# A hybrid decoder step on one core: PSUM banks lent out by the list scheduler in the order in which it places steps, the last normalisation in other tiles, longer counted durations

## The chip, the cores and the metric

The kernel runs on one core of a Trainium2 chip. The metric is device time in microseconds (us) for one execution. A core has a matrix engine (TensorE, PE in the profile, with its weight loads shown as PEld), a vector engine (VectorE, DVE), a scalar engine (ScalarE, ACT), GpSimd (POOL) and SyncE (SP), whose queue issues almost all of the transfers (DMAs) here. Matmuls write to PSUM, which has eight banks of 128 partitions by 512 float32; everything else lies in SBUF.

## The reference

One layer, 256 prompt tokens and 64 sample tokens (8 sequences of 8), model width 2048, all in float32. The tokens are normalised and projected with one large matrix (2048 by 12,416 columns); branch A is a delta-rule recurrence with 16 heads of 64, branch B a gated linear recurrence with 8 heads of 128. Cut to what matters:

```python
h = rms_norm(x, norm_g);  p = h @ w_in
sh = cur + (prev - cur) * shift_mu                       # token shift of r, k, v, wd, ad
decay = exp(-exp(-softplus(-(w0 + tanh(wd) @ w2)) - 0.5));  a = sigmoid(a0 + ad @ a2)
kk = k * k_k / |k * k_k|;  k = k * (1 + (a - 1) * k_a)
# branch A, per token and head:
S = S * w - (S kk)(kk * a)^T + v k^T ;  y = S r
y_a = ((y - mean) * rsqrt(var + GN_EPS)) * ln_w + ln_b   # the "last normalisation"
y_a = (y_a + sum(r * k * r_k) * v) * silu(p_za)
# branch B, per token and head:
S = diag(g) S + k v^T ;  o = S^T q ;  y_b = rms_norm(o) * hg_g * silu(p_zb)
merged = sigmoid(p_ga) * (y_a @ proj_a) + sigmoid(p_gb) * (y_b @ proj_b)
y = rms_norm(x + merged @ w_out) * final_g               # and all end states are returned
```

## The kernel before, in words

**Streams.** A large float32 product is made of three products of float32r parts: each weight tile of 1024 rows by 128 columns is loaded (`raw`), ScalarE rounds it to `whi`, VectorE subtracts to get `wlo`, and PE multiplies `whi` with the high and low part of the activations (`hhi`, `hlo`) and `wlo` with `hhi`. So each half tile of 128 output columns is one DMA of 512 KB, one ScalarE and one VectorE operation of 1024 columns, and 24 matmuls of 128x128 by 320 tokens, written to one of two PSUM tiles `mps`. Such matmuls are called streams below. There are three buffers each of `raw`, `whi` and `wlo`.

**Stages.** First the tokens are normalised and transposed. Then comes the recorded stage (lines 1431 to 1497): 71 tiles of `w_in` (eight for each of eight head pairs, in the order r, k, v, za, q, f, i, zb, then NFILL + NLATE = 7 gate tiles, of which the last three are stored to DRAM and fetched again later; the tile of the decay ranks is multiplied ahead of it) and, between them, the two recurrences of each pair. Then gate tiles and the two projections (lines 1524 to 1551, `ppa`, `ppb`), which need `ya` and `yb` of all pairs, split into `yah`, `yal` and so on (lines 1514 to 1523). Last the output projection (`po`) and the final norm.

**The planner.** In the recorded stage no instruction is issued when it is written. The class `Recorder` (lines 79 to 323) collects them: `add` (97) gives each a counted duration `cost` and a latency `lat` until its result can be used; `link` (179) finds who depends on whom; `order` (233) then plays the engines forward with these counts. On PE it takes a ready small step before a stream (with some rules about array modes, lines 264 to 280), on the others it takes by rank, and weight splits by due time. The resulting order is issued engine by engine (line 1496), and the framework adds the semaphores. So the chip executes each engine's list strictly in the planned order: where the plan believed a result to be ready earlier than it is, the engine stands still. Counted: a matmul's result after 215 ns plus a margin of 400 ns; a DMA 5500 ns; a DMA from or to the DRAM scratch `scr` 3300 ns, or 4600 ns if its rows have 1024 elements.

**One head pair of branch A** (`rwkv`, lines 810 to 1196). The front: decay and rate (`lora_w`, `lora_a` through `wst`, `ast` on PE), key norm (`uQ`, `uK`), a prefix sum `B` (`uB`), exponentials `ex` (`uE`) and `e2` (`uS`), products `bk2` and `arp`. Then ten matmuls of all score blocks (`arp`, `bk2`) into four PSUM tiles, masked into `g2`. A triangular inverse follows: `nd` (tag `big`) goes to DRAM (`prompt_[0]`), the sample part `dns` too (`sample_[0]`), and both come back spread over partitions, as `U` (columns 0 to 1023 of the tile `ww`) and `eighth` (columns from 1056, line 954); VectorE solves 8x8 blocks in `ww`; the result goes to DRAM (`scr<-xc`) and back (`ye`, `xt` in `uQ`, `yes`), becomes `yz`, and PE multiplies (`a<-yz,uE`, then `a<-ww,uQ`). Then four chunks run one after the other (`pr`, `pu`, `pd`, lines 1062 to 1104), the samples beside them, `py` sums the output, and the last normalisation (lines 1176 to 1196) subtracts the mean (`jr_cent`), squares, averages (`jr_mean`) and writes `ya`.

**Tiles and banks.** SBUF tiles come from `ring` (731) by tag: one buffer each, mostly. Several names share a tag: `uE` is `ex`, then `M`, then `yc` of the last normalisation; `uB` is `B`, then `sq`; `uA` is `a`, then `sg`; `uK` is `kk`, `pw_`, `yt` and `rv`; and `uS`, `uB`, `pp` lie within `ww`. Six PSUM banks are given out by the same `ring` in written order: three in turn to branch A (tag `a`), two to branch B (tag `b`), one to `y` (`own[0]`, `pr`, `py`). Of three `a` banks, the one for a product of the next pair is thus fixed by how many were asked for before it in the text.

Of the kernel before, what the change touches and what calls it, by code (L numbers as in the profile page):

```python
# [9 lines left out]
F32 = mybir.dt.float32  # L10
F32R = mybir.dt.float32r
# [3 lines left out]
PSUM = bass.MemoryType.PSUM  # L15
# [4 lines left out]
NT = NP_ + NS  # L20
# [20 lines left out]
NFILL = 4  # L41
NLATE = 3
BUFS = {"r": 1, "k": 1, "v": 1, "za": 2, "q": 2, "f": 2, "i": 1, "zb": 1}

# [5 lines left out]
class Op:  # L50
    __slots__ = ("eng", "fn", "args", "kw", "cost", "lat", "uses", "mode", "passes", "cols", "stream",
                 "succ", "npred", "ready", "rank", "block", "margin", "wait", "port", "hold", "dma", "n", "group")

# [25 lines left out]
class Recorder:  # L79
    APART, MARGIN, WAIT, OVER = 10, 400, 6000, 45  # L80
    AHEAD, SLIP = 300, 0
    LAT = {"PE": 215, "V": 40, "S": 40, "G": 65, "Y": 0}
    DRAIN = {"V": 85, "S": 100, "G": 65}

    def __init__(self, engines, is_big):
        self.real, self.ops, self.spans, self.is_big = engines, [], {}, is_big
        self.block, self.wait, self.group = None, 0, None

# [8 lines left out]
    def add(self, eng, name, fn, args, kw):  # L97
        o = Op()
# [5 lines left out]
        for d in out.shape[1:]:  # L104
            free *= d
        o.uses = []
        for j, x in enumerate(aps):
            t_ = x.tensor
            key = (t_.name, x.offset, tuple(map(tuple, x.ap)))
            if key not in self.spans:  # L110
                self.spans[key] = blocks_of(x) if t_.name.startswith("scr") else span_of(x)
            o.uses.append((*self.spans[key], j == 0, "PSUM" in str(x.space)))
# [29 lines left out]
        elif eng == "V":  # L142
            two = name in ("tensor_scalar", "tensor_copy") and all(not u[5] for u in o.uses)
            o.cost = (free / 2 if two else free) / 0.96 + (150 if two else 157)
            if two:
                o.hold = o.port = True
            if any(tuple(x.shape[1:]) == (1,) and free > 1 for x in aps[1:]):
                o.cost += 55
            if name == "tensor_tensor_scan":
                o.cost = 2 * free / 0.96 + 157  # L150
        elif eng == "S":
            o.cost = (150 if name == "copy" else 200) + free / 1.2
            if name == "copy" and not o.uses[1][5]:
                o.cost += 40
            if any(tuple(x.shape[1:]) == (1,) and free > 1 for x in aps[1:]):
                o.cost += 90 if k.get("func") == AF.Copy or AF.Copy in a else 60
        elif eng == "G":
            o.cost = 950 if "dma" in name else 95 + free * 0.88 if name == "memset" else (330 if name == "tensor_copy" and free > 9 else 200) + free * 1.66
            if "dma" in name:
                o.lat = 4500  # L160
        else:
            o.cost, o.lat = 380, 5500
            if any(u[0].startswith("scr") for u in o.uses):
                o.lat = 4600 if out.shape[-1] == 1024 else 3300
        if eng in self.DRAIN and not o.dma:
            if name == "tensor_reduce":
                n = 1
                for d in aps[1].shape[1:]:
                    n *= d
                o.cost += (n - free) / 0.96  # L170
            if out.shape[0] == 128:
                o.cost -= self.DRAIN[eng]
                o.lat += self.DRAIN[eng]
            else:
                o.cost += 13
        self.ops.append(o)
        return o

    def link(self):
# [53 lines left out]
    def order(self):  # L233
# [12 lines left out]
        at = {}  # L246
        for j, o in enumerate(bigs):
            at.setdefault(o.block, j)
        gone = run_ = 0

        def choose(e):

            q = ready[e]
            now = free[e]
            if e in port:
                held = port["G" if e == "V" else "V"] - self.OVER
                if e == "V" and held > now and port["G"] == free["G"]:

                    held += min((o.cost for o in ready["G"] if o.hold and o.ready <= free["G"] - 40), default=0.0)
                at_ = {o: max(now, o.ready, held if o.port else 0.0) for o in q}  # L260
                t_ = min(at_.values())
            else:
                t_ = max(now, min(o.ready for o in q))
            if e == "PE":
                can = [o for o in q if o.ready <= t_ + 1]
                own = [o for o in can if o.mode == mode and not o.stream]
                part = [o for o in can if o.mode != (128, 128)]
                if mode != (128, 128):
                    near = [o for o in q if o.mode == mode and o.ready <= t_ + 60]
                    pool = own or near or part or can  # L270
# [7 lines left out]
                if o.stream:  # L278
                    o = min((o for o in pool if o.stream), key=lambda o: o.n)
                return max(t_, o.ready), o  # L280
            if e not in port:
# [14 lines left out]
        while left:  # L296
            t_, o = min((choose(e) for e in ready if ready[e]), key=lambda x: (x[0], x[1].eng == "V"))
            ready[o.eng].remove(o)
# [14 lines left out]
            if o.hold:  # L313
                port[o.eng] = start + cost
            free[o.eng] = end = start + cost
            for q, data in o.succ:
                q.npred -= 1
                q.ready = max(q.ready, end + (o.lat + q.margin if data else 0))
                if not q.npred:
                    ready[q.eng].append(q)  # L320
# [4 lines left out]
def hybrid_step(ctx, tc, x_prompt, x_sample, state_rwkv, state_hgrn, state_shift, norm_g, w_in,  # L325
# [397 lines left out]
    pb = rec.enter_context(tc.tile_pool(name="pb", bufs=1))  # L723
    psa = rec.enter_context(tc.tile_pool(name="psa", bufs=1, space=PSUM))
    psb = rec.enter_context(tc.tile_pool(name="psb", bufs=1, space=PSUM))
    psy = rec.enter_context(tc.tile_pool(name="psy", bufs=1, space=PSUM))
    rings = {}
    wide_ = pa.tile([128, 1288], F32, name="ww", tag="ww")
    SHARED = {"uS": 0, "uB": 384, "pp": 768}

    def ring(pool, tag, shape, bufs, dt, size, clear=False):
# [17 lines left out]
        if len(shape) == 2:  # L749
# [3 lines left out]

    SIZES = {"uK": 384, "uS": 384, "uE": 384, "uA": 320, "uB": 384, "uQ": 320, "pp": 256, "big": 512, "s0t": 512, "v": 384,
             "w1": 384, "w2": 320, "w3": 320, "ks": 128, "ket": 256, "o": NT}
# [12 lines left out]
    def aps(name="aps"):  # L768
        return ring(psa, "a", [128, 512], 3, F32, None)

    def bps(name="bps"):
        return ring(psb, "b", [128, 512], 2, F32, None)

# [36 lines left out]
    def rwkv(p, r, k, vp, za):  # L810
# [38 lines left out]
        e = at("e", (128, 16))  # L849
        f = at("f", (128, 16))  # L850
        V.tensor_copy(e[:, 0:4], B[:, 31:NP_:64])
# [73 lines left out]
        banks = [aps("pg") for _ in HS]  # L925
        own = [ring(psy, "y", [128, 512], 1, F32, None), aps("pg")]
        side_by_side([((banks[h][:, 128 * ci:128 * ci + 128] if ci < 4 else own[h][:, :128],
# [23 lines left out]
        Y.dma_start(U, prompt_[0].rearrange("(b i) m -> b (i m)", i=32)[:, None].to_broadcast([16, 8, 1024]))  # L951
        pitch, parts_ = wide_.ap[0]
        within = lambda o_, *d: bass.AP(wide_.tensor, wide_.offset + o_, [wide_.ap[0], *d])
        eighth = bass.AP(wide_.tensor, wide_.offset + 1056, [[8 * pitch, 16], [32, 8], [1, 8]])
        Y.dma_start(eighth, sample_[0].rearrange("(b i) j -> b i j", i=8))
# [33 lines left out]
        for h in range(2):  # L989
            for a_ in range(2):  # L990
                Y.dma_start(xt[64 * h:64 * h + 32, 2 * a_:2 * a_ + 2, 0:32],
                            prompt_[1].rearrange("(a h c b r) m -> a h b r c m", a=2, h=2, c=2, b=2)[a_, h, 0])
        yes = at("yes", (64, 2, 8))
        Y.dma_start(yes, sample_[1].rearrange("(h p) j -> p h j", h=2))
# [42 lines left out]
        yh = at("yh", dt=F32R)  # L1037
        yl = at("yl", tag="rl", dt=F32R)

# [3 lines left out]
        states = []  # L1043
        pr = ring(psy, "y", [128, 512], 1, F32, None)
        psr = aps("psr")
# [16 lines left out]
        def chunks():  # L1062
            st_ = None
            for ci in range(4):
# [3 lines left out]
                if st_ is None:  # L1068
                    S.copy(rt[tk, 0], pr[HS[0], 0:64])
                    S.copy(rt[tk, 1], pr[HS[1], 0:64])  # L1070
                    rv = at("rv", (128, 3, 64), tag="uK")
                    S.copy(rv.rearrange("p c v -> p (c v)"), pr[:, 64:256])
# [83 lines left out]

        py = ring(psy, "y", [128, 512], 1, F32, None)
        work = []
# [21 lines left out]
        sums(ps[:, :NT], jr_cent, (yh, yl))  # L1180
        yc = at("yc", (128, 384), tag="uE")[:, :NT]
        S.copy(yc, ps[:, :NT])
        sq = at("sq", tag="uB")
        S.activation(sq, ps[:, :NT], AF.Square)
        sp = parts(sq)
        sg = at("sg", tag="uA")
        sigm(sg, za)
# [301 lines left out]
    with tc.manual_schedule():  # L1489
        book = Recorder({"PE": T, "V": V, "S": S, "G": G, "Y": nc.sync},  # L1490
                        lambda out: out.tensor.name.startswith("mps"))
        real = V, S, G, T
        V, S, G, T, Y = (book.proxy(e) for e in ("V", "S", "G", "PE", "Y"))
        record_all()
        V, S, G, T = real
        for o in book.order():
            o.fn(*o.args, **o.kw)  # L1497

# [217 lines left out]
```

## Time and profile before

| | |
|---|---|
| three runs | 1091.84, 1093.39, 1093.44 us; median 1093.39 us |
| the profiled execution | 1095.93 us, with a span of 1094.1 us from its first to its last instruction |
| mean granted TensorE clock | 0.995 |
| HBM read and written | 154.07 MB and 11.42 MB, 151 GB/s over the span |
| sixteen DMA engines | the hardware queue's packets take 52.4% of their time |

All times of the trace are counted from the first instruction. An engine's busy time is the union of its instructions; PE is pipelined, so that the recorded duration of a matmul is longer than the time until the next one starts. A wait is put down to whoever set the semaphore last. Inside the recorded stage nearly every instruction has line 1497, where the plan is issued; they are told apart by what they write and read: `a<-yz,uE` is a matmul that writes a PSUM tile of ring `a` and reads `yz` and `uE`.

### The profile page before, as it was taken

Reading aid. Unit: us, or ns where it says so; the run is one execution under the profiler, and the core shown is the slowest. Engines: PE = TensorE matmul, PEld = TensorE weight load, DVE = VectorE, ACT = ScalarE, POOL = GpSimd, SP = SyncE. Lnnn points to the kernel's source line nnn. Section 1 sums busy time; section 2 is a strip of 40 time slices with the busy share of each in tenths; the row PEclk is TensorE's granted clock in tenths of the full one; section 3 lists DMA queues with packets and bytes.
Section 4 is the critical chain, followed back from the end, with each engine's and each line's share of the span. In section 5 each row is a group of like instructions: output and inputs, shape, how many; then the busy total and the mean of one; then the engine's idle time right before and its main releaser. Section 6 shows DMA issues by size and latency. Waiting matters only on the chain.

```text
span 1094.1 us, 23029 instructions
## 1 busy us (share of the span) xinstructions
PE 1065.8 (97%) x8828; PEld 1027.6 (94%) x8828; DVE 760.6 (70%) x1640; ACT 706.5 (65%) x1608; POOL 133.3 (12%) x366
## 2 busy tenths in 40 slices
PE   8998999999999999999999999999999999999996
PEld 7998998998999989999989989999999999988885
DVE  8778898888897986997897885644444444446532
ACT  7757968868879959859769777544444444444412
POOL 8510120301210210300210110000000000000000
PEclk9999999999999999999999999999999999999999
DMA  6654554655555455555455555555455555587402
GB/s 197 184 146 125 154 159 121 166 145 152 144 164 141 138 163 140 138 145 159 138 145 155 140 143 164 153 155 159 144 147 154 154 146 146 152 302 247 162 20 96
DMA packets 302353, 166.98 MB, mean 153 GB/s; under 512 B 39261, under 2 KB 291424, under 8 KB 301668
## 3 DMA queue, kind: packets, MB, share of 16 engines
q1 hardware_dynamic: 301876, 164.21, 52.4%
q8 instruction: 69, 1.13, 0.4%
q10 hardware_dynamic: 368, 1.31, 0.3%
q14 instruction: 40, 0.33, 0.1%
HBM read 154.07 MB, written 11.42 MB: 151 GB/s over the span
## 4 chain that ended last, share of the span: by engine, by line
PE 78%; DVE 10%; DMA 4%; ACT 4%; issue 3%; SPq 0%; DVEq 0%; POOL 0%; ACTq 0%
PE mps L1497 30%; PE a L1497 7%; PE mps L389 5%; PE mps L391 5%; PE mps L390 5%; DVE wlo L1497 3%; DMA ww<-scr 3%; PE b L1497 3%; PE po L1589 3%; PE po L1588 3%; PE po L1587 3%; PE ppa L390 2%; PE ppb L389 2%; PE ppb L390 2%; PE ppb L391 2%
## 5 line engine op out<-in xcount | busy, mean ns | idle before, releaser
L1497 PE MATMUL mps<-hhi,wlo 128*128 128x320 f32 x1136 | 357.1, 314 | 1.5 <-DVE wlo L1497 0.8
L1497 PE MATMUL mps<-hlo,whi 128*128 128x320 f32 x1136 | 357.5, 315 | 0.0
L1497 PE MATMUL mps<-hhi,whi 128*128 128x320 f32 x1136 | 357.2, 314 | 0.0
L1497 PEld LDWEIGHTS mps<-hhi,wlo 128*128 128x128 f32 x1136 | 214.6, 189 | 2.7 <-DVE wlo L1497 1.4
L1497 PEld LDWEIGHTS mps<-hhi,whi 128*128 128x128 f32 x1136 | 214.5, 189 | 1.6 <-issue 1.2
L1497 PEld LDWEIGHTS mps<-hlo,whi 128*128 128x128 f32 x1136 | 214.4, 189 | 1.6 <-issue 0.8
L1497 DVE TENSOR_TENSOR wlo<-raw,whi 128x1024 fp32r<-128x1024 f32 x140 | 172.5, 1232 | 21.8 <-ACT whi L1497 20.6
L379 ACT CAST whi<-raw 128x1024 fp32r<-128x1024 f32 x82 | 86.2, 1051 | 147.2 <-PE mps L390 94.0
L380 DVE TENSOR_TENSOR wlo<-raw,whi 128x1024 fp32r<-128x1024 f32 x82 | 100.5, 1225 | 111.1 <-ACT whi L379 110.9
L1497 ACT CAST whi<-raw 128x1024 fp32r<-128x1024 f32 x140 | 145.8, 1043 | 42.4 <-PE mps L1497 27.2
L389 PE MATMUL mps<-hhi,whi 128*128 128x320 f32 x400 | 123.6, 309 | 0.0
L390 PE MATMUL mps<-hlo,whi 128*128 128x320 f32 x400 | 123.6, 309 | 0.0
L391 PE MATMUL mps<-hhi,wlo 128*128 128x320 f32 x400 | 123.6, 309 | 0.0
L389 PEld LDWEIGHTS mps<-hhi,whi 128*128 128x128 f32 x400 | 75.1, 188 | 0.0
L390 PEld LDWEIGHTS mps<-hlo,whi 128*128 128x128 f32 x400 | 75.1, 188 | 0.0
L391 PEld LDWEIGHTS mps<-hhi,wlo 128*128 128x128 f32 x400 | 75.1, 188 | 0.0
L1576 DVE TENSOR_TENSOR wlo<-raw,whi 128x1024 fp32r<-128x1024 f32 x32 | 38.5, 1222 | 38.0 <-ACT whi L1575 37.9
L1575 ACT CAST whi<-raw 128x1024 fp32r<-128x1024 f32 x32 | 33.3, 1053 | 47.4 <-PE po L1592 29.7
L1589 PE MATMUL po<-wlo,mhi 128*128 128x512 f32 x128 | 50.0, 391 | 0.0
L1587 PE MATMUL po<-whi,mhi 128*128 128x512 f32 x128 | 50.0, 391 | 0.0
L1588 PE MATMUL po<-whi,mlo 128*128 128x512 f32 x128 | 50.0, 391 | 0.0
L389 PE MATMUL ppa<-yah,whi 128*128 128x320 f32 x128 | 39.7, 310 | 0.5 <-ACT yah L1519 0.5
(429 smaller groups left out, 2045.8 us busy)
## 6 DMA issues: line engine op xcount, KB each, us to landing
raw<-in_w_in_dram SPq DMA_DIRECT2D x194, 512.0 KB
raw<-in_w_out_dram SPq DMA_DIRECT2D x32, 512.0 KB
raw<-in_proj_a_dram SPq DMA_DIRECT2D x16, 512.0 KB
raw<-in_proj_b_dram SPq DMA_DIRECT2D x16, 512.0 KB
s<-in_state_hgrn_dram SPq DMA_DIRECT2D x8, 512.0 KB
ww<-scr SPq DMA_DIRECT2D x8, 512.0 KB
out_dram<-s SPq DMA_DIRECT2D x8, 512.0 KB
s<-in_state_rwkv_dram SPq DMA_DIRECT2D x8, 256.0 KB
```

The lines of the kernel that those rows point to most:

```text
L379: S.copy(hi[:, ks], raw[:, ks])
L380: sub.tensor_sub(lo[:, ks], raw[:, ks], hi[:, ks].bitcast(F32))
L389: T.matmul(dst, hi[:, q, :], xhi[:, k, :], start=(k == 0), stop=False)
L390: T.matmul(dst, hi[:, q, :], xlo[:, k, :], start=False, stop=False)
L391: T.matmul(dst, lo[:, q, :], xhi[:, k, :], start=False, stop=(k == nk - 1))
L1497: o.fn(*o.args, **o.kw)
L1575: S.copy(hi, raw)
L1576: V.tensor_sub(lo, raw, hi.bitcast(F32))
L1587: T.matmul(pt, h, hi, start=first, stop=False)
L1588: T.matmul(pt, l, hi, start=False, stop=False)
L1589: T.matmul(pt, h, lo, start=False, stop=end)
```

## The change

It has three parts, all in the recorded stage.

**Banks.** The six PSUM banks are six tiles `bank0` to `bank5`. `aps` (now also `bps`, and the `y` tiles) returns no bank but a numbered loan, an address in an imaginary tensor. While `order` runs, a PE step whose loan has no bank yet can be placed only if a bank is idle: `entry` looks at the steps that ask, takes them by rank, skips those that still have an unplaced step ahead of the loan (`asked`) or that are ready only later than 1500 ns from now (`SOON`), and keeps back as many banks as a step or a side-by-side group asks for. When the step is placed, its loan gets the bank that came free first; after the loan's last step the bank is idle again. `emit` puts the real bank's address in when the instruction is issued.

**Tiles.** The last normalisation no longer uses `uE`, `uB` and `uA`: `yc` and `sq` lie in `bk`, `sg` in `big`; the rounded square reuses `yh` and `yl`, and `yl` moves from `rl` to the tag `fd`. `rv` moves from `uK` to `pp`, `yes` to `dns`, and `f` gets two buffers. `ww` grows from 1288 to 1312 columns, and `eighth` is written as a slice of the tile and no more as an address built by hand; it covers the same elements.

**Counts.** A scratch DMA counts 4500 ns and no more 3300, with 1024 elements 6500 and no more 4600. Every step of VectorE, ScalarE and GpSimd that is no DMA counts 20 ns more (`SPARE`).

The number and kind of computing instructions stay as they are, except that the split of the square is written out instead of a call of `parts`. The changed lines (those without context; the numbers are lines of the kernel before near which they stand):

```diff
@@ -40 @@
+LOAN = 128 * 512
@@ -78 @@
-    AHEAD, SLIP = 300, 0
+    AHEAD, SLIP, SOON, SPARE = 300, 0, 1500, 20
-        self.block, self.wait, self.group = None, 0, None
+        self.block, self.wait, self.group, self.loans, self.lent = None, 0, None, -1, []
@@ -103 @@
-        o.uses = []
+        o.uses, o.loans = [], set()
+            if t_.name.startswith("bank"):
+                n, off = divmod(x.offset, LOAN)
+                o.loans.add(n)
+                o.uses.append((f"loan{n}", *span_of(self.moved(x, off))[1:], j == 0, True))
+                continue
@@ -161 @@
-                o.lat = 4600 if out.shape[-1] == 1024 else 3300
+                o.lat = 6500 if out.shape[-1] == 1024 else 4500
+            o.cost += self.SPARE
@@ -175 @@
+    def moved(self, x, off, home=None):
+        home = home or self.lent[0]
+        return bass.AP(home.tensor, home.offset + off, [list(d) for d in x.ap])
+    def emit(self, o):
+        def real(x):
+            if not (hasattr(x, "tensor") and x.tensor.name.startswith("bank")):
+                return x
+            n, off = divmod(x.offset, LOAN)
+            return self.moved(x, off, self.lent[self.home[n]])
+        o.fn(*(real(x) for x in o.args), **{k: real(x) for k, x in o.kw.items()})
@@ -247 @@
+        open_, needs, until = {}, {}, {}
+        for o in self.ops:
+            for n in o.loans:
+                open_[n] = open_.get(n, 0) + 1
+                until[n] = 0.0
+        members = {}
+        for o in self.ops:
+            if o.group is not None:
+                members.setdefault(o.group, set()).update(o.loans)
+        for o in self.ops:
+            for n in o.loans:
+                needs.setdefault(n, o.loans if o.group is None else members[o.group])
+        own, before = {}, {}
+        for o in self.ops:
+            for q, _ in o.succ:
+                before.setdefault(q.n, []).append(o.n)
+            for n in o.loans:
+                own.setdefault(min(needs[n]), set()).add(o.n)
+        ahead, asked = {}, {}
+        for key, mine in own.items():
+            top = max(mine)
+            past, todo = set(), list(mine)
+            while todo:
+                for q, _ in self.ops[todo.pop()].succ:
+                    if q.n <= top and q.n not in past:
+                        past.add(q.n)
+                        todo.append(q.n)
+            todo = list(mine)
+            inner = set(mine)
+            while todo:
+                for n in before.get(todo.pop(), ()):
+                    if n in past and n not in inner:
+                        inner.add(n)
+                        todo.append(n)
+            outer = {n for m in inner for n in before.get(m, ())} - inner
+            asked[key] = len(outer)
+            for n in outer:
+                ahead.setdefault(n, []).append(key)
+        idle = [(0.0, j) for j in range(len(self.lent))]
+        self.home = {}
+        def wanted(o):
+            return [n for n in (o.loans if o.group is None else members[o.group]) if n not in self.home]
+        def entry(q, now):
+            at_, asking = {}, {}
+            for o in q:
+                want = wanted(o)
+                if not want:
+                    at_[o] = o.ready
+                elif not asked[min(needs[want[0]])]:
+                    asking.setdefault(min(want), []).append(o)
+            room, rooms = len(idle), sorted(idle)
+            for some in sorted(asking.values(), key=lambda s_: max((o.rank, -o.n) for o in s_), reverse=True):
+                n = len(wanted(some[0]))
+                first = min(o.ready for o in some)
+                if first > now + self.SOON:
+                    continue
+                if n <= room:
+                    for o in some:
+                        at_[o] = max(o.ready, rooms[n - 1][0] + o.margin)
+                room -= n
+            return at_
-            if e in port:
+            if e == "PE":
+                at_ = entry(q, now) or entry(q, 1e9)
+                q = list(at_)
+                if not q:
+                    return None
+                t_ = max(now, min(at_[o] for o in q))
+            elif e in port:
@@ -262 @@
-                can = [o for o in q if o.ready <= t_ + 1]
+                can = [o for o in q if at_[o] <= t_ + 1]
-                    near = [o for o in q if o.mode == mode and o.ready <= t_ + 60]
+                    near = [o for o in q if o.mode == mode and at_[o] <= t_ + 60]
@@ -277 @@
-                return max(t_, o.ready), o
+                return max(t_, at_[o]), o
@@ -294 @@
-            t_, o = min((choose(e) for e in ready if ready[e]), key=lambda x: (x[0], x[1].eng == "V"))
+            t_, o = min(filter(None, (choose(e) for e in ready if ready[e])), key=lambda x: (x[0], x[1].eng == "V"))
+            for n in wanted(o):
+                idle.sort()
+                self.home[n] = idle.pop(0)[1]
@@ -313 @@
+            for key in ahead.get(o.n, ()):
+                asked[key] -= 1
+            for n in o.loans:
+                open_[n] -= 1
+                until[n] = max(until[n], end + o.lat)
+                if not open_[n]:
+                    idle.append((until[n], self.home[n]))
@@ -721 @@
-    psa = rec.enter_context(tc.tile_pool(name="psa", bufs=1, space=PSUM))
-    psb = rec.enter_context(tc.tile_pool(name="psb", bufs=1, space=PSUM))
-    psy = rec.enter_context(tc.tile_pool(name="psy", bufs=1, space=PSUM))
+    psl = rec.enter_context(tc.tile_pool(name="psl", bufs=1, space=PSUM))
+    lent = [psl.tile([128, 512], F32, name=f"bank{j}", tag=f"bank{j}") for j in range(6)]
-    wide_ = pa.tile([128, 1288], F32, name="ww", tag="ww")
+    wide_ = pa.tile([128, 1312], F32, name="ww", tag="ww")
@@ -751 @@
-    SIZES = {"uK": 384, "uS": 384, "uE": 384, "uA": 320, "uB": 384, "uQ": 320, "pp": 256, "big": 512, "s0t": 512, "v": 384,
+    SIZES = {"uK": 384, "uS": 384, "uE": 384, "uA": 320, "uB": 384, "uQ": 320, "pp": 256, "fd": NT, "big": 512, "s0t": 512, "v": 384,
@@ -766 @@
-        return ring(psa, "a", [128, 512], 3, F32, None)
-    def bps(name="bps"):
-        return ring(psb, "b", [128, 512], 2, F32, None)
+        book.loans += 1
+        at_ = lent[0]
+        return bass.AP(at_.tensor, at_.offset + book.loans * LOAN, [list(d_) for d_ in at_.ap])
+    bps = aps
@@ -847 @@
-        f = at("f", (128, 16))
+        f = at("f", (128, 16), bufs=2)
@@ -923 @@
-        own = [ring(psy, "y", [128, 512], 1, F32, None), aps("pg")]
+        own = [aps("py"), aps("pg")]
@@ -949 @@
-        pitch, parts_ = wide_.ap[0]
-        eighth = bass.AP(wide_.tensor, wide_.offset + 1056, [[8 * pitch, 16], [32, 8], [1, 8]])
+        eighth = wide_[0:128:8, 1056:1312].rearrange("p (i x) -> p i x", x=32)[:, :, 0:8]
@@ -990 @@
-        yes = at("yes", (64, 2, 8))
+        yes = at("yes", (64, 2, 8), tag="dns")
@@ -1035 @@
-        yl = at("yl", tag="rl", dt=F32R)
+        yl = at("yl", tag="fd", dt=F32R)
-        pr = ring(psy, "y", [128, 512], 1, F32, None)
+        pr = aps("py")
@@ -1068 @@
-                    rv = at("rv", (128, 3, 64), tag="uK")
+                    rv = at("rv", (128, 3, 64), tag="pp")
@@ -1154 @@
-        py = ring(psy, "y", [128, 512], 1, F32, None)
+        py = aps("py")
@@ -1178 @@
-        yc = at("yc", (128, 384), tag="uE")[:, :NT]
+        ends = bk.rearrange("p c k -> p (c k)")
+        yc, sq = ends[:, :NT], ends[:, NT:2 * NT]
-        sq = at("sq", tag="uB")
-        sp = parts(sq)
-        sg = at("sg", tag="uA")
+        S.copy(yh, sq)
+        V.tensor_sub(yl, sq, yh.bitcast(F32))
+        sp = yh, yl
+        sg = at("sg", tag="big")
@@ -1490 @@
+        book.lent = lent
-            o.fn(*o.args, **o.kw)
+            book.emit(o)
```

More of the change, by code (lines that the diff above doesn't have):

```diff
@@ L51 @@
     __slots__ = ("eng", "fn", "args", "kw", "cost", "lat", "uses", "mode", "passes", "cols", "stream",
-                 "succ", "npred", "ready", "rank", "block", "margin", "wait", "port", "hold", "dma", "n", "group")
+                 "loans", "succ", "npred", "ready", "rank", "block", "margin", "wait", "port", "hold", "dma", "n", "group")
 def span_of(ap):
```

## The prediction

> **What bounds the kernel now.** I read the page first, then the busy time of each engine in the three parts of the run, then PE's waits in the recorded stage, then each wait's surroundings in the timeline.
>
> ```profile
> span 1094.1 us, 23029 instructions
> PE 1065.8 (97%) x8828; PEld 1027.6 (94%) x8828; DVE 760.6 (70%) x1640; ACT 706.5 (65%) x1608; POOL 133.3 (12%) x366
> ```
>
> ```profile
> 0.00:28.70 28.70, 23.54 (x130) 21.49 (x131) 23.57 (x51) 21.29 (x40) 23.43 (x54) 1.00 0.63 189
> 28.70:678.00 649.30, 635.68 (x6187) 619.58 (x6186) 542.37 (x1343) 507.60 (x1300) 109.84 (x313) 0.99 0.54 149
> 678.00:1094.10 416.10, 406.54 (x2515) 386.53 (x2513) 194.69 (x247) 177.60 (x268) 0.00 (x0) 1.00 0.51 156
> ```
>
> The columns after the length are the busy times of PE, PEld, DVE, ACT and POOL. The change touches the middle part alone, from 28.7 to 678.0 us. There PE works 635.68 of 649.30 us, and VectorE is next with 542.37, so PE bounds the stage. The change removes no matmul, so what it can win here is PE's idle time, 649.30 - 635.68 = 13.6 us, and what hangs on it. Who causes it:
>
> ```profile
> PE a L1497 <- ACT yz L1497: 7.9, 4, 2.9
> PE a L1497 <- DVE rl L1497: 1.6, 1, 1.6
> PE a L1497 <- DVE bks L1497: 1.4, 1, 1.4
> PE mps L1497 <- DVE wlo L1497: 0.8, 1, 0.8
> PE a L1497 <- POOL yz L1497: 0.8, 1, 0.8
> PE mps L1497 <- issue: 0.6, 1, 0.6
> PE a L1497 <- DVE st L1497: 0.2, 1, 0.2
> ```
>
> Each row is waiter, releaser, total, number, longest. In eight of these ten single waits PE stands at a small step (`a`) whose vector or scalar operand comes late, five times at the first product after the inverse's way through DRAM (`yz`: 7.9 + 0.8 = 8.7 us). These are not shortages of streams. PE's list put a small step there because the plan counted its operand as ready; the chip, which can't reorder, waits. The plan is too early, and by how much shows at pair 0:
>
> ```profile
> 68.24 0.57 SPq L1497 DMA_DIRECT2D ww<-scr  x1
> 73.79 0.53 SPq L1497 DMA_DIRECT2D ww<-scrs  x1
> ...
> 77.19 0.19 DVE L1497 TENSOR_TENSOR big<-ww 128x30 f32<-128x30 f32 x1 [3.02 <-DMA ww<-scrs]
> 96.32 0.68 PE L1497 MATMUL a<-yz,uE 128*128 128x128 f32 x4 [2.93 <-ACT yz L1497]
> 404.62 1.19 PE L1497 MATMUL a<-yz,uE 128*128 128x128 f32 x4 [2.42 <-ACT yz L1497]
> ```
>
> ```profile
> SPq L1497 <- DMA ww<-scr: 40.9, 8, 6.0
> ```
>
> `U` is issued at 68.24; `eighth` leaves only at 73.79, because SP waits for `U` to land (40.9 / 8 = 5.1 us for each pair, with the later weight loads queued behind it), though the two fill different columns. The first solve starts at 77.19, 77.19 - 68.24 = 9.0 us after `U` was issued. The plan counts 380 + 4600 ns = 5.0 us there. It is 4.0 us early, and PE's wait of 2.93 us at 96.32 is what is left of that.
>
> **Waits long enough also cost clock.**
>
> ```profile
> 97.00:100.45 3.45, 3.45 (x15) 3.25 (x14) 3.32 (x13) 1.39 (x5) 0.17 (x1) 0.51 0.73 213
> 404.20:407.65 3.45, 3.02 (x12) 3.06 (x13) 3.11 (x8) 1.70 (x6) 0.40 (x2) 0.51 0.43 130
> ```
>
> Around the two longest waits (2.93 and 2.42 us) the granted clock is 0.51 for 3.45 us. That loses (1 - 0.51) times PE's busy 3.45 and 3.02 us: 1.7 + 1.5 = 3.2 us. After the shorter waits (up to 1.6 us) nothing of the kind shows, so I count these 3.2 us as hanging on the long ones. That they have another cause is a rival below.
>
> **Are the pairs serial?** This decides whether PE, freed of waits, still has streams to do.
>
> ```profile
> 120.12 0.31 PE L1497 MATMUL a<-yh,jr_cent 128*128 128x320 f32 x1
> 120.82 0.31 PE L1497 MATMUL a<-lora_w,wst 128*128 128x320 f32 x1
> ```
>
> ```profile
> L1497 SPq DMA_DIRECT2D scr<-big x32: 327/422/434, 63.5 to 608.5; - x32
> L1497 DVE SCALAR_TENSOR_TENSOR v<-dif,cols,pad x16: 274/379/504, 53.1 to 566.0; 128x256 f32<-128x256 f32 x8, 128x64 f32<-128x64 f32 x8
> L1497 DVE TENSOR_TENSOR ya<-uE,uA x8: 491/492/495, 126.7 to 678.3; 128x320 f32<-128x320 f32 x8
> POOL uE L1497 <- DVE ya L1497: 38.7, 7, 9.2
> ```
>
> Pair 1's first product (`lora_w`) comes 0.7 us after pair 0's last normalisation began (`jr_cent`): the `a` bank in turn is free only then. Its `ex` waits further for pair 0's `ya`, since both use `uE` (GpSimd waits 38.7 us in seven times). So a pair starts when the one before ends. The inverse's DMAs recur every (608.5 - 1.3 - 63.5) / 7 = 77.7 us (1.3 us for the three issues of 0.42 us between a pair's first and last), the input v every (566.0 - 0.4 - 53.1) / 7 = 73.2 us. The chain of pairs is 4.5 us a pair slower than the streams, and falls behind them by 32 us over the stage. The seven gate tiles at the end are the cover, used up to the last: the last `ya` starts at 678.3, and the last stream has started by 678.0, where the stage is cut. If PE's idle time went and the chain stayed, PE would only wait at the end. Both must go together.
>
> **The change part by part.**
>
> *Counts.* The way through DRAM counts four scratch DMAs in a row (`nd` out, `U` in, `xc` out, `ye` in): 1.9 + 3 x 1.2 = 5.5 us more. The plan was 4.0 us early, so the product with `yz` should now be placed behind enough streams that its operand is there; the streams in between hide this. I take the 8.7 us of `yz` waits down to 1.0: -7.7. The five other causes (1.6 + 1.4 + 0.8 + 0.6 + 0.2 = 4.6 us) were operands late by 0.2 to 1.6 us. 20 ns for each of the some dozens of steps in a row before them are about that size, so half goes: -2.3. With the two long waits the slow clock goes: -3.2. What the counts cost: the 20 ns on 1343 VectorE steps make 26.9 us, 542.37 + 26.9 = 569 of 649 us in the plan, still below PE, so no wait of PE is planned for VectorE's sake.
>
> *Banks and tiles.* They let pair p+1's front run beside pair p's tail: `ex`, `B`, `a` and `kk` are no longer held by `yc`, `sq`, `sg`, `rv`, and no bank is fixed by the text. What still holds pair p+1 back is `arp`, `g2` and `uv`, which pair p reads until `py`, just ahead of 120.12. Now the scores go out as `nd` some 77.7 - (120.12 - 63.5) = 21 us after that. If only `arp` and the ten matmuls have to follow, I estimate a gain of 10 us, and 4.5 are enough to keep pace with the streams. This gives nothing by itself: it is what lets the sum above be collected at the end.
>
> *New waits.* A bank's next writer waits for its last reader, and the order of loans rests on counted times. In the list above no wait is for a bank. The bounds are 0 and the 8.7 us that the plan's worst error costs now; two pairs interleaved are new, but the nearest row is 0, so I take +2.0. How often PE changes between small steps and streams may shift either way: of PE's 635.68 us, 16.1 have no weight load beside them (619.58), and a fifth of that, 3 us, bounds it on both sides. I take 0.
>
> *`eighth` as a slice.* If the framework now sees that it is apart from `U`, SP no longer stands still for 5.1 us, and the solves start about 3.4 us earlier (77.19 - 73.79, its own landing). If not, all stays. It is off the bound either way, as long as the pairs overlap: 0, with a wait of PE of up to 9.0 - (0.38 + 6.5) = 2.1 us a pair if it stays. The 1.0 above takes half a chance of a part of that.
>
> *After the stage.* PE's first projection waits 0.5 and 0.4 us for the split of `ya`, itself behind the last gate tile's store. That stays: 0.
>
> ```profile
> PE ppa L389 <- ACT yah L1519: 0.5, 1, 0.5
> PE ppa L390 <- DVE yal L1520: 0.4, 1, 0.4
> 685.10 2.61 ACT L1519 CAST yah<-ya 128x640 fp32r<-128x640 f32 x4 [2.33 <-DMA scrg<-f]
> ```
>
> **Sum:** -7.7 - 2.3 - 3.2 + 2.0 = -11.2 us. The profiled execution (1095.93, 1.8 us outside its span) would become 1084.7; it is 2.5 us above the median, so the median of 1093.39 becomes 1082.2.
>
> **Rivals.**
>
> *The slow clock stays (6%).* The two stretches may have a cause of their own and come again: the gain is 3.2 us smaller, 1085.4. For it: two cases are few. Against it: both begin within 1 us of the end of the two longest waits of the stage (96.32, 404.62). [...]
>
> *Half (15%).* `eighth` still waits for `U` and four pairs still wait about 1 us at `yz`, or new bank waits take 4 us more than I count: about -6, 1087.4. For it: SP's wait is the framework's doing, not the plan's.
>
> *Waits only move (11%).* The plan is changed everywhere, and its errors show up at other places for the same 13.6 us: 1093.4. For it: the waits by `rl`, `bks` and `st` have nothing to do with scratch DMAs. Against it: they are a third of the idle time.
>
> *The chain gets longer (14%).* If the pairs remain serial, by `arp`, `g2` and `uv`, each pair is planned 5.5 us later, 4.0 of which the chip needed anyway; 1.5 us a pair, and about 2 us for some hundred steps of a pair at 20 ns, make 3.5 x 8 = 28 us at the last `ya`, with the streams used up: 1121. It decides once pair p+1 wins less than 3.5 us by starting earlier. Against it: 38.7 us of waiting for `uE` alone goes, and the `lora_w` row shows the front waiting for a bank. [...]
>
> **The numbers.** My forecast has 54% (1077 to 1087). If all 13.6 + 3.2 + 0.9 us went, it would be 1075.7, the low end; the high end, 1093, takes in the half gain and part of no change, and leaves out the longer chain and a rest of no change. A measurement of this kernel can tell 0.2% (2.2 us) from no change. Faster: 54 + 6 + 15 = 75%; same 11%; slower 14%.
>
> **What would show it.** Right: PE idle below 5 us in the recorded stage, no clock of 0.5 in it, `lora_w` of pair p+1 on PE well ahead of pair p's `jr_cent`, the inverse's DMAs every 73 to 75 us, and the last `ya` some us ahead of the last gate tile. Wrong: PE waiting for a reader of a bank, a gap at the end of the stage before `ppa`, or `yz` waits as before.

## The result and the profile after

The changed kernel takes 1078.66 us (median of four runs, 1077.21 to 1080.13) against 1093.41 us, a ratio of 0.9867, 95% interval 0.9848 to 0.9885. That is 14.75 us less; 11.2 were forecast.

Busy time of each engine in the three parts of the changed kernel (after the length: PE, PEld, DVE, ACT, POOL, granted clock, DMA share, GB/s):

```profile
0.00:26.80 26.80, 20.86 (x130) 18.30 (x131) 23.18 (x51) 20.65 (x37) 24.44 (x54) 1.00 0.68 202
26.80:661.30 634.50, 630.12 (x6188) 618.15 (x6187) 541.64 (x1344) 504.96 (x1304) 98.21 (x313) 1.00 0.56 151
661.30:1077.50 416.20, 406.92 (x2515) 386.45 (x2513) 195.01 (x246) 177.56 (x268) 0.00 (x0) 0.99 0.52 157
```

The recorded stage went from 649.30 to 634.50 us, 14.8 less. The last part is the same (416.10 and 416.20). The first is 1.9 us shorter, which isn't the change: the stage begins at 26.8 to 27.9 in every other run told of here, with the old planner too; the profiled run of before had a late start. Of the 14.8 us, 9.2 are PE's idle time (13.6 to 4.4) and 5.6 its busy time. PE's waits in the stage:

```profile
PE bank L198 <- issue: 3.4, 2, 2.1
PE bank L198 <- ACT rhs L198: 0.6, 2, 0.3
PE bank L198 <- POOL fd L198: 0.4, 1, 0.4
```

```profile
99.74 0.25 PE L198 MATMUL bank<-uv,g 128*32 128x64 f32 x2 [0.30 <-ACT rhs L198]
```

All rows of `yz`, `rl`, `bks`, `wlo` and `st` are gone. The two waits behind `rhs`, 0.6 us in all, are for a bank's reader: the matmul `bank<-uv,g` waits until ScalarE's copy `rhs<-bank` is done, and it doesn't read `rhs`. Most of what is left stands in the first row: two waits for which the profile has no releaser (the last section says what they go with). Behind the longer one (2.15 us) clock is lost too, as this stretch of the windows view shows after the wait that ends at 330.49:

```profile
330.49 0.22 PE L198 MATMUL bank<-ket 128*32 128x32 f32 x2 [2.15 <-issue]
```

```profile
330.90:334.30 3.40, 3.40 (x15) 3.40 (x16) 1.51 (x8) 1.68 (x7) 0.00 (x0) 0.50 0.02 5
```

Half of 3.40 us, 1.7, is lost there; before it was 3.2. So 1.5 of the 5.6 us of busy time are clock. For the other 4.1 the profile names nothing. Recorded matmuls overlap (a small one of 0.27 us starts 0.11 us after the one before), so by my estimate an operand late by 0.1 us can delay and yet leave no idle time behind; I take the 4.1 us for such waits, but no view shows them one by one. How often PE changes between streams and small steps is not the cause: by the matmul records of the stage it does so 570 times before and 576 times after.

The pairs, in PE's timeline and in the rows by tile:

```profile
83.00 0.31 PE L198 MATMUL bank<-lora_w,wst 128*128 128x320 f32 x1
124.53 0.40 PE L198 MATMUL bank<-yh,jr_cent 128*128 128x320 f32 x1
```

```profile
L198 SPq DMA_DIRECT2D scr<-big x32: 327/424/1462, 59.8 to 590.9; - x32
L198 DVE SCALAR_TENSOR_TENSOR v<-dif,cols,pad x16: 265/376/486, 59.5 to 577.8; 128x64 f32<-128x64 f32 x8, 128x256 f32<-128x256 f32 x8
L198 DVE TENSOR_TENSOR ya<-bk,big x8: 481/491/734, 132.2 to 658.3; 128x320 f32<-128x320 f32 x8
```

Pair 1's first product now comes 41.5 us ahead of pair 0's last normalisation, where it came 0.7 us after it. The inverses recur every (590.9 - 1.3 - 59.8) / 7 = 75.7 us (77.7 before), and the last `ya` starts 3 us before the stage ends. And at pair 0 SP no longer stands between the two transfers, and the first solve starts 7.5 us after `U` is issued instead of 9.0 (SP's and VectorE's timelines):

```profile
64.83 0.56 SPq L198 DMA_DIRECT2D ww<-scr  x1
65.45 0.59 SPq L198 DMA_DIRECT2D ww<-scrs  x1
...
72.36 0.18 DVE L198 TENSOR_TENSOR big<-ww 128x30 f32<-128x30 f32 x1
```

It is not sooner in every pair: over all eight the first solve starts on average 8.7 us after `U` is issued, and 8.0 before; in seven of the eight VectorE works without a pause until the solve begins, so the plan and not the landing sets the time.

### The profile page after: what moved, and what is told of

The parts are those of the page before. It is cut to its first block, busy times and chain, and to the rows that moved or that the text cites. A ratio compares the mean times of both kernels' runs of the same rounds, so it can differ in the third digit from the quotient of the medians.

```text
span 1077.5 us, 23000 instructions
## 1 busy us (share of the span) xinstructions
PE 1057.9 (98%) x8828; PEld 1022.9 (95%) x8828; DVE 759.8 (71%) x1640; ACT 703.2 (65%) x1608; POOL 122.6 (11%) x366
## 4 chain that ended last, share of the span: by engine, by line
PE 96%; DVE 1%; ACT 1%; issue 1%; DMA 1%; POOL 0%; DVEq 0%; ACTq 0%
PE mps L198 47%; PE bank L198 11%; PE mps L493 5%; PE mps L492 5%; PE mps L491 5%; PE po L1693 3%; PE po L1691 3%; PE po L1692 3%; PE ppb L492 2%; PE ppb L493 2%; PE ppb L491 2%; PE ppa L493 2%; PE ppa L492 2%; PE ppa L491 2%; PE po L1697 1%; PE po L1696 1%
## 5 line engine op out<-in xcount | busy, mean ns | idle before, releaser
L492 PE MATMUL ppa<-yal,whi 128*128 128x320 f32 x128 | 39.6, 310 | 0.4 <-DVE yal L1624 0.4
```

The source lines that it names most:

```text
L492: T.matmul(dst, hi[:, q, :], xlo[:, k, :], start=False, stop=False)
```

## The experiments

The theory: the longer counts take PE's waits away, and lent banks with new tiles let the pairs overlap, so that this can be collected. The rivals: the counts do it alone, or the overlap does. Each run has its own runs of the kernel before beside it on the same chip, so ratios are what can be compared between rows. "Period" is that of the inverses, from each run's own row of `scr<-big`.

| run | banks | tiles | 20 ns | scratch counts | `ww` | us | ratio (95%) | period |
|---|---|---|---|---|---|---|---|---|
| before | turns | old | no | old | 1288 | 1093.41 | 1 | 77.7 |
| changed | lent | new | yes | long | 1312 | 1078.66 | 0.9867 (0.9848, 0.9885) | 75.7 |
| e1 | turns | old | yes | long | 1288 | 1134.62 | 1.0376 (1.0361, 1.0392) | 84.3 |
| e2 | lent | new | no | old | 1312 | 1087.07 | 0.9940 (0.9924, 0.9957) | 74.1 |
| e3 | lent | old | yes | long | 1312 | 1116.82 | 1.0217 (1.0202, 1.0232) | 82.6 |
| e4 | turns | new | yes | long | 1312 | 1121.62 | 1.0256 (1.0240, 1.0271) | 82.1 |
| e5 | turns | old | no | old | 1312, slice | 1084.78 | 0.9929 (0.9907, 0.9950) | 76.5 |
| e6 | lent | new | yes | long | 1312, by hand | 1077.75 | 0.9862 (0.9845, 0.9878) | 75.3 |
| e7 | lent | new | no | long | 1312 | 1082.60 | 0.9903 (0.9888, 0.9918) | 74.0 |
| e8 | lent | new | yes | 3000 ns longer | 1312 | 1122.30 | 1.0262 (1.0238, 1.0286) | 83.4 |
| e9 | turns | old | no | old | 1312, by hand | 1084.87 | 0.9923 (0.9906, 0.9940) | 76.6 |
| e10 | lent | new | yes | long | 1288, by hand | 1077.27 | 0.9855 (0.9840, 0.9870) | 75.4 |
| e11 | lent | new | yes | old | 1312 | 1074.57 | 0.9836 (0.9818, 0.9853) | 73.8 |
| e12 | turns | old | yes | old | 1312, by hand | 1104.30 | 1.0070 (1.0053, 1.0088) | 79.4 |

### The counts alone (e1)

```diff
 # the kernel before
-                o.lat = 4600 if out.shape[-1] == 1024 else 3300
+                o.lat = 6500 if out.shape[-1] == 1024 else 4500
         if eng in self.DRAIN and not o.dma:
+            o.cost += self.SPARE        # 20
```

> The kernel before with the longer counts alone (scratch DMAs 6500 and 4500, 20 ns a step); banks, tiles and the hand-built address of eighth as before. My theory (the counts take the waits away, the overlap of the pairs lets the gain be collected): the waits at yz are gone, but the pairs stay serial and each is some 3.5 us longer, so the last ya comes up to 28 us later and PE idles at the end of the recorded stage: 1095 to 1121 us. Rival 'counts do it all': 1079 to 1082 us, with no wait at the end. Rival 'overlap does it all': 1093 us or a little more, the yz waits as before.

It takes 1134.62 us, beyond the slow end of my own range. PE's waits and the inverses:

```profile
PE mps L1498 <- ACT pad L1498: 24.9, 5, 8.9
PE a L1498 <- DVE rl L1498: 10.1, 2, 7.4
```

```profile
L1498 SPq DMA_DIRECT2D scr<-big x32: 306/424/1245, 61.7 to 652.9; - x32
```

The `yz` waits are gone from the list, but the period is 84.3 us. The idle time isn't at the end, as I had it, but in the middle: a stream can't begin because the PSUM tile that it needs hasn't been copied out to `pad`. With r, k and v in one buffer each, the copy waits for the pair before, so streams run dry in five of the eight pairs. The counts alone lose 41 us.

### The overlap without the counts (e2), without the scratch counts (e11), without the 20 ns (e7)

```diff
 # the changed kernel; e11 has the first edit, e7 the second, e2 both
-                o.lat = 6500 if out.shape[-1] == 1024 else 4500
+                o.lat = 4600 if out.shape[-1] == 1024 else 3300
-    AHEAD, SLIP, SOON, SPARE = 300, 0, 1500, 20
+    AHEAD, SLIP, SOON, SPARE = 300, 0, 1500, 0
```

> The changed kernel with the old counts (4600 and 3300, no 20 ns); banks lent and new tiles stay. My theory: the pairs overlap as in the changed kernel (inverse every 75 to 76 us), but the plan is too early again at yz, PE idles 8 to 13 us in the stage: 1084 to 1091 us. Rival 'overlap does it all': within 0.2% of the changed kernel, 1077 to 1081 us. Rival 'counts do it all': 1091 to 1095 us.

> The changed kernel without the 20 ns a step (scratch DMAs stay at 6500 and 4500). My theory: between the changed kernel and the one with all old counts (1087), nearer to the latter if the many small late operands are what the counts mend: 1082 to 1087 us. If the scratch DMAs' counts are what matters: 1077 to 1081 us.

> The changed kernel with the scratch DMAs' old counts (4600 and 3300), the 20 ns a step stay. The 20 ns alone were worth 4 us (1082.6 without them) and all counts together 8.4 (1087.1). If the two add up: 1081 to 1085 us. If, with eighth free of U, the old scratch counts are long enough and the longer ones only lengthen the chain: 1074 to 1079 us.

The two counts don't add up. By the ratios, with the old scratch counts the 20 ns are worth 1.04% of the time of before (0.9940 to 0.9836; 1% is 11 us), with the long ones 0.36% (0.9903 to 0.9867). The long scratch counts gain 0.37% without the 20 ns and cost 0.31% with them. So the fastest of all, 1074.57, has the scratch counts of before; its interval and the changed kernel's just touch. The stage in e2 and in e11:

```profile
26.80:669.80 643.00, 635.27 (x6189) 618.85 (x6188) 542.14 (x1344) 509.75 (x1305) 108.52 (x313) 1.00 0.54 150
```

```profile
26.80:656.50 629.70, 628.61 (x6187) 616.36 (x6187) 542.87 (x1344) 506.77 (x1305) 102.65 (x313) 1.00 0.56 153
```

In both the pairs keep well ahead (74.1 and 73.8 us). In e11 PE idles 1.1 us in the stage, against 4.4 in the changed kernel. Those 3.3 us and the 1.7 of clock make up the 4.8 us by which e11's stage is shorter, and both come from the waits without a releaser (3.4 against 0.2 us). So this shows the long scratch counts to be unnecessary, not that they lengthen anything by themselves. In e2 the loss is not at `yz`, as I had expected (0.2 us there): 6.6 us of idle time more than e11, 4.9 of it waits without a releaser (5.1 and 0.2 us), and 6.7 us of longer busy time, 1.7 of them clock (an estimate, worked out in the last section). So about half of what the 20 ns are worth here (4.9 and 1.7 of 13.3 us in the stage) hangs on waits for which the profile names no late operand. Since only 20 ns was run, it is not shown how much of it another count, or another order, would bring.

### Banks or tiles alone (e3, e4)

```diff
 # e3: the changed kernel with the tiles of before, for instance
+        yc = at("yc", (128, 384), tag="uE")[:, :NT]
-        yc, sq = ends[:, :NT], ends[:, NT:2 * NT]
 # e4: the kernel before with the new tiles, slice and counts; its banks stay
         return ring(psa, "a", [128, 512], 3, F32, None)
```

> The changed kernel with the last normalisation, rv, yl, yes and f back in the tiles of before; banks lent, slice and longer counts stay. My theory: lora_w of the next pair still comes ahead of jr_cent, but its ex waits for ya through uE, so the pairs are about as serial as before and longer: last ya behind the last gate tile, 1085 to 1110 us. If the banks are the whole of the overlap: 1077 to 1081 us.

> The kernel before with the new tiles, the slice and the longer counts, but the banks by turns in written order. My theory: lora_w of the next pair comes only around jr_cent, the front can't run beside the tail, so 1085 to 1105 us with PE idle at the end of the stage. If the tiles are the whole of the overlap: 1077 to 1081 us.

Both are slower than before, by 2.2% and 2.6%, and beyond the slow end of my ranges. Neither half of the overlap is any good without the other while the long counts stand. In e4 PE waits like this, in e3 the same for 16.2 us:

```profile
PE mps L1499 <- ACT pad L1499: 14.9, 5, 7.3
```

### The wait of `eighth` (e5, e6, e9, e10)

```diff
 # e9: the kernel before, one number; e5: this and eighth as a slice
-    wide_ = pa.tile([128, 1288], F32, name="ww", tag="ww")
+    wide_ = pa.tile([128, 1312], F32, name="ww", tag="ww")
 # e6: the changed kernel; e10: this and 1288 columns
-        eighth = wide_[0:128:8, 1056:1312].rearrange("p (i x) -> p i x", x=32)[:, :, 0:8]
+        eighth = bass.AP(wide_.tensor, wide_.offset + 1056, [[8 * wide_.ap[0][0], 16], [32, 8], [1, 8]])
```

> The kernel before with eighth written as a slice of ww (ww widened to 1312 columns) and nothing else. SP should no longer wait for U to land ahead of eighth, and the solves start about 3.4 us earlier in each pair, with the old plan. My theory: a true latency taken off a serial chain shows even without the other parts; the yz waits of 8.7 us and the two slow stretches of 3.2 us mostly go, 1081 to 1088 us. Rival 'off the bound': SP's wait costs nothing and the plan sets the pace, within 0.2% of before, 1091 to 1095.5 us.

> The changed kernel with the address of eighth built by hand again (the wide ww stays). SP waits about 5 us for U in each pair again. My theory: the longer counts cover most of it, and the pairs overlap: PE waits up to 2 us a pair at yz, 1079 to 1087 us. Rival 'off the bound': within 0.2% of the changed kernel, 1077 to 1081 us.

> The kernel before with ww 1312 columns wide and nothing else: the address of eighth is still built by hand, the plan's order is the same. In the run with the changed kernel and the hand-built address SP did not wait for U, so the cause of the wait would be the width (the pattern of 8 rows of 32 from column 1056 ends at 1312), not the way of writing it. Then SP's wait is gone and the time is that of the slice alone, 1082 to 1088 us. If the slice is what frees it: SP's wait of 5 us stays, 1091 to 1095.5 us.

> The changed kernel with ww 1288 columns wide and the hand-built address, so with the false wait back: the solves start some 3 us later in each pair. My theory now: lent banks and new tiles run the pairs side by side and the longer counts cover the late solves, so PE waits little at yz: 1078 to 1084 us. If the freed wait is the main part of the gain: 1084 to 1092 us.

e5 gives 0.9929: a true latency off a serial chain is worth 8 us with no change to the plan. e6 was to bring SP's wait back and did not, so the slice isn't what frees it. e9 changes the width alone, and that is enough (0.9923). SP's and VectorE's timelines in e9:

```profile
66.49 0.57 SPq L1497 DMA_DIRECT2D ww<-scr  x1
67.18 0.53 SPq L1497 DMA_DIRECT2D ww<-scrs  x1
...
72.90 0.19 DVE L1497 TENSOR_TENSOR big<-ww 128x30 f32<-128x30 f32 x1 [0.49 <-DMA ww<-scrs]
```

```profile
PE a L1497 <- ACT yz L1497: 1.9, 3, 1.1
```

The instructions of all engines are those of the kernel before in the same order, and the wait of 40.9 us in eight is gone: 6.4 us from `U` to the first solve at pair 0 instead of 9.0, and 1.9 us of `yz` waits instead of 8.7. The pattern of eight rows of 32 columns from column 1056 ends at 1312; in a tile of 1288 columns it reaches past the row's end, and the framework then takes it to overlap with `U`. That last step is argued; that the width decides is shown.

In the changed kernel none of this matters: e10, with the old width, is as fast as with the new one (1077.27 us, just below my range). Its waits of SP and its timeline at pair 1 say why:

```profile
SPq L198 <- DMA ww<-scr: 4.1, 1, 4.1
```

```profile
136.61 0.54 SPq L198 DMA_DIRECT2D ww<-scrs  x1
137.25 2.10 SPq L198 DMA_DIRECT2D raw<-in_w_in_dram  x2
139.58 0.55 SPq L198 DMA_DIRECT2D ww<-scr  x1
```

The plan issues `eighth` ahead of `U` in seven of eight pairs, so there is one wait where there were eight. Lent banks and new tiles together bring this order, not the longer count: e2, with neither count, has it in seven pairs too, and in e1, e3 and e4, which have the longer counts but at most one of the two, `U` is first in all eight. By which step of the plan they do it, no run shows.

### Longer counts still (e8), and the 20 ns on serial pairs (e12)

```diff
 # e8: the changed kernel
-                o.lat = 6500 if out.shape[-1] == 1024 else 4500
+                o.lat = 9500 if out.shape[-1] == 1024 else 7500
 # e12: e9 with the 20 ns
+            o.cost += self.SPARE
```

> The changed kernel with still longer scratch DMAs: 9500 with 1024 elements, 7500 else, 3 us more for each of four in a row, 12 us a pair. My theory: with the chain already as slow as the streams (last ya 3 us ahead of the last gate tile), 12 us more a pair make the chain the bound, streams run out in the middle of the stage: 1095 to 1150 us. If overlapped pairs hide a longer chain: 1077 to 1083 us.

> The kernel before with ww 1312 columns wide and 20 ns more a step, scratch DMAs counted as before (4600 and 3300); banks by turns and the tiles as before. It is the same as the fastest so far (1074.6: lent banks, new tiles, 20 ns, old scratch counts) less the lent banks and the new tiles. My theory: the pairs are serial and 20 ns for each step make the planned chain about 2 us a pair longer than the 77 us that it has with the width alone, so streams run dry late in the stage and the time is 1085 to 1105 us. If banks and tiles are not needed once the false wait is gone: 1073 to 1079 us.

e8 is the slow rival come true in the changed kernel: 83.4 us a pair, streams waiting for the copy of `zb`, and the projection waiting for the last `ya`:

```profile
PE mps L198 <- ACT zb L198: 9.6, 5, 3.1
PE ppa L491 <- ACT yah L1623: 4.9, 1, 4.9
```

e12 settles what the overlap (lent banks and new tiles together) is for. Serial pairs with the freed wait lose by the 20 ns (0.9923 to 1.0070, 76.6 to 79.4 us a pair), and overlapped ones gain by them (e2 to e11, 0.9940 to 0.9836).

```profile
PE mps L1498 <- ACT pad L1498: 8.1, 2, 5.6
```

## Why the prediction was right, point by point

**The bound and the waits.** Right. PE's idle time in the stage was to fall by 8.0 us net and fell by 9.2; all `yz` waits went (1.0 was left to them), and of the five others' 4.6 us 1.0 is left, at other steps.

**New waits, +2.0.** The size was near (3.4 us), but by luck, since the kind was wrong: they are the waits without a releaser, which the prediction didn't have. For a bank's reader there are 0.6 us, which are among the 1.0 us just named.

**Clock, -3.2.** 1.5 came. The two stretches after the `yz` waits went with them, which speaks against the rival that they stay; a new one follows a new wait. With it one of the signs named for a right prediction failed (no clock of 0.5), and a second one narrowly: the inverses recur every 75.7 us, not every 73 to 75.

**Changes between small steps and streams, 0 within 3 us.** Too narrow: PE's busy time fell by 4.1 us beside the clock, the time without a weight load beside it from 16.1 to 12.0. The number of changes isn't why (570 and 576), so the sum had no term for these 4.1 us. Together with 1.2 us more of idle time and 1.7 less of clock than forecast they are the difference between -11.2 and -14.8.

**The overlap gives nothing by itself and is needed to collect the rest.** Right for the counts, and the experiments show it more sharply than I put it: banks and tiles with the old counts and the new width, e2, are no faster than the width alone, e9; without banks, tiles or both the counts lose 24 to 41 us. But not all of the gain needs the overlap: the width alone takes 6.8 of the 8.7 us of `yz` waits away on serial pairs. I had the idle time of a slow chain at the end of the stage; it lies in the middle, where streams wait for the copy into a tile that the pair before still holds.

**The slow rival** has its point: the chain decides once a pair takes longer than its streams. At 79.4 us (e12) and 82 to 84 us (e1, e3, e4, e8) all runs are slower than before, at 74 to 77 none is.

**`-7.7` by the scratch counts.** Longer counts can do this, since e1 has no `yz` row, but they aren't needed. e11 has no `yz` wait with the old ones, and e2, with neither count, has 0.2 us: with `eighth` free and the pairs overlapped, 4600 and 3300 ns are enough. The old count was also less wrong than pair 0 made it look: its 9.0 us from `U` to the first solve are the longest of the eight, and the others take 6.6 to 8.6.

**`eighth`, 0.** Right in the changed kernel (e10, with the old width, lies within its interval), but for a reason that I didn't have, the new order on SP. On the serial pairs of before, for which the prediction gave no figure, it is worth 8 us, and its cause is a width, not the way of writing the address.

## What to carry to other kernels

Where a plan is made ahead, a wait of the bounding engine for a small step is a wrong count or a wait that the plan doesn't know: look in the issuing queue for the latter first, since here one tile's width alone, on the kernel before, was worth 8.2 of the 14.75 us. Longer counts are safe only as long as the chain that they lengthen has slack against the bounding engine's own work; compare the period of both before and after, and make the chain overlap (buffers and banks together) before the counts are raised. Test each count by itself with the others in place: here the larger of them was superfluous.

## What the runs showed of the hardware

In bursts of matmuls of 32 columns PE stands still with no releaser in the profile, for 1.22 and 2.15 us in the changed kernel and 1.84 us in e9, and once in the streams behind such a burst (0.59 us, ending at 179.73 in the kernel before); the longest such wait of all runs is 2.4 us (e12). Where the order on PE is the same, in the changed kernel, e6 and e10, it does so at the same two matmuls (here e6 and e10):

```profile
252.28 0.19 PE L198 MATMUL bank<-o 128*32 128x32 f32 x1 [1.22 <-issue]
329.31 0.22 PE L198 MATMUL bank<-ket 128*32 128x32 f32 x2 [1.02 <-issue]
```

```profile
252.68 0.19 PE L198 MATMUL bank<-o 128*32 128x32 f32 x1 [1.67 <-issue]
330.30 0.22 PE L198 MATMUL bank<-ket 128*32 128x32 f32 x2 [1.60 <-issue]
```

Such waits go with the packets of a queue that the pages of before, of the changed kernel and of e1 to e4 list with the same figures:

```profile
q8 instruction: 69, 1.13, 0.4%
```

That is 69 packets of 16 KB, one for every 256 of PE's 8828 matmuls and 8828 weight loads, in the changed kernel some 15.6 us apart on average. Their pace follows PE's: 49 fall in its recorded stage, one for every 253 of 12,375 matmuls and loads, and 19 in the part behind it, one for every 265 of 5,028. So I take them for PE's own instructions; the page doesn't say whose they are. In the packet records of before and of the changed kernel, from 25 us on, PE has three waits of more than 0.4 us without a releaser (0.59, 1.22 and 2.15 us), and they end 1.41, 1.24 and 1.59 us after such a packet has landed; the 12 waits of that length with a named releaser end 2.2 to 20.3 us after one. The matmuls of such a burst start about every 13 ns (twelve from 330.49 to 330.65 in the changed kernel's timeline; streams are some 150 ns apart), so by an estimate 128 of them with their weight loads use up a packet in 1.7 us, while in these three cases 2.3 to 2.7 us pass from the start of a packet to the end of the wait. That PE waits there for its own instructions is my estimate from these numbers; no run moved the bursts or the packets on purpose.

The granted clock was 0.50 for 3.40 us after the wait of 2.15 us (the changed kernel, 330.90 to 334.30), and streams one behind the other started 0.27 us apart there, against 0.15 elsewhere. After the 1.84 us of e9, which end at 98.45, they start 0.27 us apart too (100.06 to 100.86), and after the 1.67 and 1.60 us of e10 0.15 us. e2 has waits of 2.3 and 2.0 us and, by an estimate, one such stretch: its mean granted clock of 0.996 over 1085.5 us is 3.8 to 4.9 us lost, of which one stretch takes 1.7; the end of the run took 1.9 us in the kernel before and 2.9 in the changed one, which leaves no room for a second. By that estimate the length of a wait alone doesn't decide it in these runs.
